# A decoder layer's feed-forward: f sums made on VectorE, operand loads further ahead, and some up-projection weights in pairs of slots

## The chip, the cores and the metric
One core of a Trainium2 chip runs the whole kernel. The metric is the device time of one execution in microseconds (us), median of several runs. The engines are named as in the profile: PE (TensorE matmul), PEld (its weight loads), DVE (VectorE), ACT (ScalarE), POOL (GpSimd, here mostly an issuer of DMAs) and SP (SyncE, here only an issuer of DMAs).

## The reference
One decoder layer on 512 tokens, model width 2048, all in float32. Its last part is what the change touches:

```
x = x + gate_a * mixers(h)                        # attention part, not touched
h = RMSNorm(x) * (1 + scale_f) + shift_f
u = h @ w_up                                      # 2048 -> 2 x 5632
conv = b_conv + sum_j w_conv[j] * shift(u, 2 - j) # causal, three taps
f = silu(conv[:, :5632]) * conv[:, 5632:]
out = x + gate_f * (f @ w_down)                   # 5632 -> 2048
```

## The kernel before
Activations lie feature-major: a tile has 128 features on the partitions and the 512 tokens as columns. Every float32 factor is split into a high and a low part in float32r (`split`: ACT copies into hi, line 114; DVE subtracts, lo = x - hi, line 115), and a product is three matmuls: hi by hi, hi by lo, lo by hi.

**The seven products.** Most of both projections goes through `seven` (lines 919 to 1055). A "pair" of output tiles is computed as a 2x2 block product in seven products in place of eight, on four weight blocks (11, 21, 22, 12) and seven operand sets of the activations (`r11 t3 t2 r21 t1 t4 r22`), each 256 tokens wide. One product is one step of `3*K` matmuls of 128x128 by 128x256: K = 8 in the up projection, 6 or 5 in the down projection. The steps run in the order p1, p7, p6, p2, p5, p4, p3. A step's preparation (`p1` and so on) is emitted two steps ahead of its matmuls: load weight blocks (SP, line 930), combine them (DVE, `comb`, line 941), split the result into one of three hi/lo buffers. After the matmuls an `e` function empties the bank: e1, e7, e6, e3 copy on ACT (`copy`, line 949 in the up projection, 947 in the down projection), e2, e5, e4 add on DVE (`plus`, lines 955 and 953). PE accumulates over several steps in one bank, so PE's p4 and p3 wait for e2 and e5. In program order the weight blocks and s3, the temporary of p7, come out of a queue of five raw buffers (`rawq`): a pair takes L11, L21, s3, L22, L12 and gives s3 back first, then L11 and L21 (p5), L22 (p4), L12 (p3). So L21 of a pair is loaded into the buffer that held L11 of the pair before, and L22 into the one that held L22.

The order of instructions on each engine is not the program's order alone: a scheduler with a model of the engines places an instruction where it believes its inputs to be there. On the chip each engine then works through its queue in that order, and so does SP with the DMAs that it issues.

**Up projection and f.** Four blocks of f are made directly, then 40 pairs by `seven` (`work`, line 1498). After a pair, `ffn_out` applies the convolution (ACT line 1340, DVE lines 1341 and 1342), silu and the product (DVE line 1435) and calls `f_out` (line 1352), which stores what the seven operand sets of the down projection need. Per two blocks j, j+1 it makes negated copies on ACT (lines 1362, 1372) and issues 14 DMAs of 128 KB on POOL: seven plain stores (lines 1363 to 1367, 1373, 1374) and seven that add in DRAM (line 1359).

**Down projection.** It runs in four stages c = 0 to 3 of 6, 6, 5, 5 K-blocks (`DH`), eight pairs each. A stage needs seven operand sets, which `load_set` (line 1448) loads from DRAM on SP (line 1454) and `split_set` (line 1457) splits. `ahead(left)` is called after every step, and it decides when: it splits if `2*need + 8` slots are free, and it keeps at most two sets loaded. A set takes three slots when loaded and six when split. All these tiles, as well as the tiles of the `e` functions and of `f_out`, come from one pool of 81 slots of 128x512 in first-in first-out order (`get`, `put`); during the up projection 64 of them hold h and its sums. Stages 0 to 2 add their result to x1 in DRAM (POOL, line 1506). In stage 3 x1 is loaded (line 1514, `plus()` of `down_pair`), DVE adds it while emptying the bank (line 945), and SP stores the output (line 1508).

Of the kernel before, what the change touches and what calls it, by code (L numbers as in the profile page):

```python
# [10 lines left out]
F32 = mybir.dt.float32  # L11
# [20 lines left out]
def trunk_layer_kernel(  # L32
# [880 lines left out]
    class Pair:  # L913


        def __init__(self, rs, load, fin, K=KH, scale=None, plus=None):
            self.rs, self.load, self.fin, self.K, self.scale, self.plus = rs, load, fin, K, scale, plus

    def seven(work, pairs_of_banks, hook=None):
        def pair_steps(n, p):  # L920
            bx, by = pairs_of_banks[n % len(pairs_of_banks)]
            X, Y, Z = bx[:, :HT], by[:, :HT], by[:, HT:]
            L, E = {}, {}
            W = p.K * P
            g1, g2 = p.scale or (None, None)
            r11, r21, r22, t1, t2, t3, t4 = p.rs

            def load(blk):
                t = rawq.popleft()
                SP.dma_start(t[:, :W], p.load(blk))  # L930
                return t

            def hilo(t):
                i = cnt["wt"] % NH
                cnt["wt"] += 1
                hi, lo = hi_b[i][:, :W], lo_b[i][:, :W]
                split(hi, lo, t[:, :W])
                return hi, lo

            def comb(o, a, b, op):  # L940
                V.tensor_tensor(o[:, :W], a[:, :W], b[:, :W], op)  # L941

            def copy(o, b, g, x):
                if x is not None:
                    V.scalar_tensor_tensor(o, b, g, x, op0=ALU.mult, op1=ALU.add)
                elif g is not None:
                    A.activation(o, b, AF.Copy, scale=g)  # L947
                else:
                    A.activation(o, b, AF.Copy)

            def plus(o, b, g, x):
                if g is not None:
                    V.scalar_tensor_tensor(o, b, g, x, op0=ALU.mult, op1=ALU.add)
                else:
                    V.tensor_tensor(o, b, x, ALU.add)  # L955

            def p1():
                L[11] = load(0)
                L[21] = load(1)
                x = p.plus() if p.plus else (None, None)  # L960
                E["x"] = x
                for i in range(2):
                    for h in range(2):
                        E[f"x{i + 1}{h}"] = None if x[i] is None else x[i][:, h * HT:(h + 1) * HT]
                return hilo(L[11])

            def p7():
                s3 = rawq.popleft()
                comb(s3, L[21], L[11], ALU.subtract)
                r = hilo(s3)  # L970
                rawq.append(s3)
                L[22] = load(3)
                return r

            def p6():
                comb(L[21], L[21], L[22], ALU.add)
                comb(L[11], L[21], L[11], ALU.subtract)
                r = hilo(L[11])
                L[12] = load(2)
                return r  # L980

            def p2():
                return hilo(L[12])

            def p5():
                r = hilo(L[21])
                comb(L[12], L[12], L[11], ALU.subtract)
                rawq.append(L[11])
                rawq.append(L[21])
                return r  # L990

            def p4():
                r = hilo(L[22])
                rawq.append(L[22])
                return r

            def p3():
                r = hilo(L[12])
                rawq.append(L[12])
                return r  # L1000

            def e1():
                E["s"] = get()
                copy(E["s"][:, :HT], X, g1, E["x10"])

            def e7():
                copy(E["s"][:, HT:], Y, g2, E["x21"])

            def e6():
                E["s6"] = get()  # L1010
                copy(E["s6"][:, :HT], X, g2, E["x20"])

            def e2():
                E["u1"] = get()
                plus(E["u1"][:, :HT], Z, g1, E["s"][:, :HT])

            def e5():
                E["u2"] = get()
                plus(E["u2"][:, HT:], X, g2, E["s"][:, HT:])
                put(E["s"])  # L1020

            def e4():
                plus(E["u2"][:, :HT], Y, g2, E["s6"][:, :HT])
                put(E["s6"])

            def e3():
                copy(E["u1"][:, HT:], X, g1, E["x11"])
                if p.plus:
                    put(*E["x"])
# [317 lines left out]


    KINDS = ("r11", "t3", "t2", "r21", "t1", "t4", "r22")
    f_d = {n: [dram.tile([P, HT], F32, name=f"f{n}_{i}") for i in range(NF_ // 2)] for n in KINDS}  # L1350

    def f_out(j, t):
        i = j // 2
        q1, q2 = t[:, :HT], t[:, HT:]
        neg = get()
        n1, n2 = neg[:, :HT], neg[:, HT:]

        def add(n, v):
            G.dma_start(f_d[n][i], v, accum_op=ALU.add)

        if j % 2 == 0:
            A.activation(neg, t, AF.Copy, scale=-1.0)
            G.dma_start(f_d["t1"][i], q2)
            G.dma_start(f_d["t4"][i], q2)
            G.dma_start(f_d["t2"][i], q1)
            G.dma_start(f_d["t3"][i], q2)
            G.dma_start(f_d["r11"][i], q1)
            add("t1", n1)
            add("t4", n1)
            add("t2", n2)  # L1370
        else:
            A.activation(n2, q2, AF.Copy, scale=-1.0)
            G.dma_start(f_d["r21"][i], q1)
            G.dma_start(f_d["r22"][i], q2)
            add("t4", q1)
            add("t2", q2)
            add("t3", n2)
            add("t4", n2)
        put(t, neg)


    tsum = [[], [], [], []]
# [65 lines left out]
    def load_set():  # L1448
        c, n = todo.popleft()
        ts = []  # L1450
        for i in range(DH[c]):
            if i % 2 == 0:
                ts.append(get())
            SP.dma_start(ts[-1][:, (i % 2) * HT:(i % 2 + 1) * HT], f_d[n][base[c] + i])
        coming.append((c, n, ts))

    def split_set():
# [21 lines left out]

    SPARE = 8  # L1480

    def up_hook(q, n):
        last = q - (n - 7)
        if last == 0:
            for t in h2[:KH]:
                put(*t)
        elif last in (1, 2, 4, 5):
            for t in tsum[{1: 2, 2: 1, 4: 0, 5: 3}[last]]:
                put(*t)
        elif last == 6:  # L1490
            for t in h2[KH:]:
                put(*t)
        ahead(n - q)


    all_banks = [(bank[2 * i], bank[2 * i + 1]) for i in range(4)]
    rs = operands(h2, tsum)
    work = [Pair(rs, lambda blk, i=i: w_ups[i, blk], ffn_out(i)) for i in range(NF_ - 4)]
    n_up = len(work) * 7

    def down_pair(c, j):
        def fin(u1, u2):
            for i, u in enumerate((u1, u2)):
                n = 2 * j + i
                if c < len(DH) - 1:
                    G.dma_start(x1_d[n], u, accum_op=ALU.add)  # L1506
                else:
                    SP.dma_start(out[n * P:(n + 1) * P, :], u)
            put(u1, u2)

        def plus():
            ts = [get(), get()]
            for i in range(2):
                G.dma_start(ts[i], x1_d[2 * j + i])
            return ts

        o = ops[c]
        return Pair(tuple(o[n] for n in ("r11", "r21", "r22", "t1", "t2", "t3", "t4")),
                    lambda blk: w_downs[c][j, blk], fin, K=DH[c],
                    scale=(mod[:, 80 + 2 * j:81 + 2 * j], mod[:, 81 + 2 * j:82 + 2 * j]),  # L1520
                    plus=plus if c == len(DH) - 1 else None)

    work += [down_pair(c, j) for c in range(len(DH)) for j in range(KD // 2)]

    def hook(q, n):
# [3 lines left out]
        c, r = divmod(q - n_up, 56)  # L1529
        if r >= 49:  # L1530
            put(*held_by[c][KINDS[r - 49]])
        ahead(0 if (coming or todo or [(0,)])[0][0] == c else 56 - r)

    seven(work, all_banks, hook)

# [55 lines left out]
```

## Time and profile before

| what | value |
|---|---|
| median of 3 runs | 2755.28 us (2752.21 to 2761.14) |
| the profiled execution | 2751.13 us, of which the traced span is 2749.4 us |
| mean granted TensorE clock in it | 0.986 of full speed |
| busy share of the span: PE, DVE, ACT, POOL | 96%, 78%, 46%, 16% |
| moved by DMA | 484.52 MB, of it 112.83 MB on the queue that POOL issues to |

Times in the views count from the start of the span. A row of the timeline has start, duration, engine, line, operation, output<-input and count; in square brackets stands how long the engine was idle ahead of it and what ended that. A row of the groups has the count after x, then total busy time, the mean of one in ns, and after the bar the idle time ahead of such instructions. A row of the waits has who waited for whom, total us, times, longest us. Durations of neighbouring instructions on one engine overlap somewhat; the spacing of their starts is what each costs in the queue.

### The profile page before, as it was taken

How to read it: one execution, taken by the hardware profiler on the slowest of the kernel's cores; microseconds unless marked ns; L12 is line 12 of the kernel's file. 1: busy time of each engine (PE TensorE's matmuls, PEld its weight loads, DVE VectorE, ACT ScalarE, POOL GpSimd, SP SyncE). 2: the span in 40 equal slices, each digit the busy share in tenths (PEclk: the TensorE clock that was granted, in tenths of full speed). 3: DMA queues.
4: the chain of work that ended last, by engine and by line, in shares of the span. 5: the costliest groups of instructions: out<-in, count | busy, mean ns of one | idle time of the engine just before them, and what ended most of it. 6: DMA issues, size and time to landing. Idle time of an engine off the chain costs nothing.

```text
span 2749.4 us, 45335 instructions
## 1 busy us (share of the span) xinstructions
PE 2633.1 (96%) x17200; PEld 2360.8 (86%) x17200; DVE 2154.1 (78%) x3427; ACT 1278.1 (46%) x1979; POOL 443.2 (16%) x715
## 2 busy tenths in 40 slices
PE   6999999998999999999999999999999989898999
PEld 5777687778997767788789999999999988898989
DVE  7977967698888658863868888888888887777788
ACT  4333434334454465222644555555555564545443
POOL 1001011110032222100132222222222221010120
PEclk8999999999999999999999999999999999999999
DMA  9943137665685588952355555555556576656674
GB/s 340 340 146 104 29 113 219 206 196 161 200 257 163 191 261 293 335 169 92 131 142 150 142 152 148 143 157 142 142 156 165 144 218 144 181 138 166 140 203 128
DMA packets 254574, 484.52 MB, mean 176 GB/s; under 512 B 27306, under 2 KB 108100, under 8 KB 254356
## 3 DMA queue, kind: packets, MB, share of 16 engines
q1 hardware_dynamic: 194452, 368.79, 42.9%
q0 software_dynamic: 59872, 112.83, 16.8%
q8 instruction: 134, 2.20, 0.3%
q14 instruction: 84, 0.69, 0.1%
q10 hardware_dynamic: 32, 0.01, 0.0%
HBM read 397.11 MB, written 84.41 MB: 175 GB/s over the span
## 4 chain that ended last, share of the span: by engine, by line
PE 56%; issue 19%; DMA 13%; DVE 9%; POOL 2%; ACT 2%; SPq 0%; DVEq 0%; POOLq 0%; ACTq 0%
PE bank L118 9%; PE bank L119 9%; PE bank L120 9%; PE bank L1050 8%; PE bank L1051 8%; PE bank L1052 8%; DMA raw<-in_w_ups 6%; DVE wlo L115 3%; DMA slot<-in_w_ada 2%; DVE raw L941 2%; POOL x L1506 1%; DMA raw<-in_w_ada 1%; ACT whi L114 1%; DMA gate<-slot 1%; PE bank L1194 1%
## 5 line engine op out<-in xcount | busy, mean ns | idle before, releaser
L1050 PE MATMUL bank<-slot,whi 128*128 128x256 f32 x3920 | 1116.0, 285 | 77.9 <-ACT slot L947 27.9
L1051 PE MATMUL bank<-slot,whi 128*128 128x256 f32 x3920 | 1108.1, 283 | 0.4 <-DVE slot L115 0.4
L1052 PE MATMUL bank<-slot,wlo 128*128 128x256 f32 x3920 | 1100.2, 283 | 2.0 <-DVE wlo L115 2.0
L1050 PEld LDWEIGHTS bank<-slot,whi 128*128 128x128 f32 x3920 | 746.7, 191 | 95.9 <-DVE slot L955 36.0
L114 ACT ACTIVATE whi<-raw 128x1024 fp32r<-128x1024 f32 (+2 forms) x560 | 531.8, 951 | 561.6 <-PE bank L1051 386.4
L1051 PEld LDWEIGHTS bank<-slot,whi 128*128 128x128 f32 x3920 | 745.1, 190 | 0.7 <-DVE slot L115 0.6
L1052 PEld LDWEIGHTS bank<-slot,wlo 128*128 128x128 f32 x3920 | 741.9, 190 | 2.8 <-DVE wlo L115 2.6
L115 DVE TENSOR_TENSOR wlo<-raw,whi 128x1024 fp32r<-128x1024 f32 (+2 forms) x560 | 606.8, 1086 | 80.4 <-ACT whi L114 78.0
L941 DVE TENSOR_TENSOR raw<-raw,raw 128x1024 f32<-128x1024 f32 (+2 forms) x320 | 348.5, 1089 | 143.9 <-DMA raw<-in_w_ups 109.6
L106 ACT ACTIVATE whi<-raw 128x1024 fp32r<-128x1024 f32 (+4 forms) x182 | 187.4, 1031 | 397.1 <-PE bank L120 205.8
L107 DVE TENSOR_TENSOR wlo<-raw,whi 128x1024 fp32r<-128x1024 f32 (+4 forms) x182 | 215.7, 1186 | 145.3 <-ACT whi L106 143.4
L119 PE MATMUL bank<-wlo,slot 128*128 128x512 f32 (+2 forms) x768 | 297.6, 388 | 0.9 <-DVE wlo L107 0.9
L118 PE MATMUL bank<-whi,slot 128*128 128x512 f32 (+2 forms) x768 | 290.3, 391 | 4.4 <-ACT slot L385 3.9
L120 PE MATMUL bank<-whi,slot 128*128 128x512 f32 (+2 forms) x768 | 293.3, 386 | 0.0
L118 PE MATMUL bank<-slot,whi 128*128 128x512 f32 (+1 forms) x656 | 261.2, 405 | 3.1 <-ACT slot L1331 2.3
L119 PE MATMUL bank<-slot,whi 128*128 128x512 f32 (+1 forms) x656 | 263.1, 402 | 0.7 <-DVE slot L687 0.7
L120 PE MATMUL bank<-slot,wlo 128*128 128x512 f32 (+1 forms) x656 | 257.7, 401 | 0.0
L118 PEld LDWEIGHTS bank<-whi,slot 128*128 128x128 f32 x768 | 146.0, 190 | 35.8 <-ACT slot L385 4.0
L723 DVE SCALAR_TENSOR_TENSOR slot<-slot,c_act,slot 128x512 f32<-128x512 f32 x203 | 149.0, 746 | 32.6 <-DMA slot<-in_w_ada 31.4
L119 PEld LDWEIGHTS bank<-wlo,slot 128*128 128x128 f32 x768 | 146.3, 191 | 30.0 <-DVE wlo L107 1.4
L120 PEld LDWEIGHTS bank<-whi,slot 128*128 128x128 f32 x768 | 144.9, 189 | 29.2 <-issue 0.5
L118 PEld LDWEIGHTS bank<-slot,whi 128*128 128x128 f32 (+1 forms) x656 | 123.2, 188 | 33.9 <-issue 2.8
(292 smaller groups left out, 2813.2 us busy)
## 6 DMA issues: line engine op xcount, KB each, us to landing
slot<-in_w_ada SPq DMA_DIRECT2D x344, 256.0 KB, 5.5
raw<-in_w_ups SPq DMA_DIRECT2D x160, 512.0 KB, 4.4
ft<-slot POOLq DMA_DIRECT2D x242, 128.0 KB, 4.6
raw<-in_w_in SPq DMA_DIRECT2D x50, 512.0 KB, 3.6
raw<-in_w_down SPq DMA_DIRECT2D x64, 384.0 KB, 3.9
raw<-in_w_down SPq DMA_DIRECT2D x64, 320.0 KB, 3.0
raw<-in_w_gs SPq DMA_DIRECT2D x32, 512.0 KB, 3.8
raw<-in_w_o SPq DMA_DIRECT2D x32, 512.0 KB, 4.7
```

The costliest lines, as they stand in the source:

```text
L106: A.activation(hi, raw[:, :w], AF.Copy)
L107: V.tensor_tensor(lo, raw[:, :w], r32(hi), ALU.subtract)
L114: A.activation(dst_hi, src, AF.Copy)
L115: V.tensor_tensor(dst_lo, src, r32(dst_hi), ALU.subtract)
L118: PE.matmul(o, lh, rh, start=first, stop=False)
L119: PE.matmul(o, lh, rl, start=False, stop=False)
L120: PE.matmul(o, ll, rh, start=False, stop=last)
L723: V.scalar_tensor_tensor(acc, ts[i], c_act[:, k:k + 1], acc, op0=ALU.mult, op1=ALU.add)
L941: V.tensor_tensor(o[:, :W], a[:, :W], b[:, :W], op)
L1050: PE.matmul(o, wh[:, ks], rh, start=first and k == 0, stop=False, skip_group_check=True)
L1051: PE.matmul(o, wh[:, ks], rl, start=False, stop=False, skip_group_check=True)
L1052: PE.matmul(o, wl[:, ks], rh, start=False, stop=last, skip_group_check=True)
```

## The change
Four things change, all in the last part of the kernel.

1. `f_out` keeps the first of two blocks in its slot, and at the second makes the four needed sums on DVE (four subtractions of 128x256). It then stores plainly: one DMA of 128 KB at the first block, three of 256 KB at the second. The negated copies on ACT and the DMAs that add go. The loads pick their half out of the wider tiles.
2. `ahead`: of a coming stage's sets up to three are loaded ahead of their split (one only, in stage 0 while 15 or fewer slots are free); it begins 50 steps ahead instead of 35. Sets are split early every fourth step, at most four, and otherwise in the last eight steps. Sets of stage c+2 no longer start within stage c. The spare count is 6 for stage 0, 8 otherwise.
3. For the first 34 of the 40 pairs of the up projection (`slots=i < NF_ - 10`), s3 and L12 live in two slots of 512 columns each, and no longer in a raw buffer. What is done on them (the load, two of the four combinations, three of the seven splits) becomes two instructions of half the width. L11, L21 and L22 stay in the five raw buffers.
4. In stage 3 the `e` functions copy on ACT as in the other stages, and two DVE additions of 128x512 per pair add x1 in `fin`.

```
     def f_out(j, b):
         i = j // 2
         if j % 2 == 0:
             first_of.append(b)
             G.dma_start(f_d[i][0], b[:, :HT])
             return
         a = first_of.pop()
         p, q = get(), get()
         V.tensor_tensor(p[:, :HT], a[:, HT:], a[:, :HT], ALU.subtract)
         V.tensor_tensor(p[:, HT:], b[:, HT:], p[:, :HT], ALU.subtract)
         V.tensor_tensor(q[:, :HT], a[:, HT:], b[:, HT:], ALU.subtract)
         V.tensor_tensor(q[:, HT:], b[:, :HT], p[:, HT:], ALU.subtract)
         for n, t in ((1, b), (2, p), (3, q)):
             G.dma_start(f_d[i][n], t)
         put(a, b, p, q)
```
```
-    def ahead(left):
-        c = todo[0][0] if todo else coming[0][0] if coming else None
-        if c is None or left > 35 or left > 8 and left % 2:
+    made = [0]
+    def ahead(left, last):
+        c = (coming or todo or [(9,)])[0][0]
+        if c > last or left > 50:
             return
-        if coming and len(free) >= 2 * need(coming[0][0]) + SPARE:
+        n, spare = need(c), 8 if c else 6
+        if coming and coming[0][0] <= c and len(free) >= 2 * n + spare and (left <= 8 or left % 4 == 0 and made[0] < 4):
+            made[0] = (made[0] + 1) % 7
             split_set()
-        if todo and todo[0][0] <= c and len(coming) < 2 and len(free) >= need(todo[0][0]) + SPARE:
+        while todo and todo[0][0] <= c and len(coming) < (3 if c or len(free) > 15 else 1) and len(free) >= n + spare:
             load_set()
```
```
             def p7():
-                s3 = rawq.popleft()
+                s3 = new(p.slots)
                 comb(s3, L[21], L[11], ALU.subtract)
                 r = hilo(s3)
-                rawq.append(s3)
+                done(s3)
                 L[22] = load(3)
...
-                L[12] = load(2)
+                L[12] = load(2, p.slots)
```
```
+        def fin(*us):
+            for i, (n, u) in enumerate(zip(ns, us)):
+                if x1:
+                    V.tensor_tensor(u, u, x1[i], ALU.add)
+                    SP.dma_start(out[n * P:(n + 1) * P, :], u)
+                else:
                     G.dma_start(x1_d[n], u, accum_op=ALU.add)
```

More of the change, by code (lines that the diff above doesn't have):

```diff
@@ L926, in pair_steps, with new, done, part @@
             r11, r21, r22, t1, t2, t3, t4 = p.rs
-            def load(blk):
-                t = rawq.popleft()
-                SP.dma_start(t[:, :W], p.load(blk))
+            def new(slots=False):
+                if slots:
+                    return [(get(), 0, T), (get(), T, W)]
+                return [(rawq.popleft(), 0, W)]
+            def done(t):
+                if len(t) == 1:
+                    rawq.append(t[0][0])
+                else:
+                    put(*(x[0] for x in t))
+            def part(t, lo, hi):
+                for b, x, y in t:
+                    if x <= lo and hi <= y:
+                        return b[:, lo - x:hi - x]
+            def cuts(*ts):
+                return [(x, y) for _, x, y in max(ts, key=len)]
+            def load(blk, slots=False):
+                t = new(slots)
+                for b, x, y in t:
+                    SP.dma_start(b[:, :y - x], p.load(blk)[:, x:y])
                 return t
@@ L936, in hilo, with copy @@
                 hi, lo = hi_b[i][:, :W], lo_b[i][:, :W]
-                split(hi, lo, t[:, :W])
+                for x, y in cuts(t):
+                    split(hi[:, x:y], lo[:, x:y], part(t, x, y))
                 return hi, lo
             def comb(o, a, b, op):
[L941 to L946, printed above, removed]
+                for x, y in cuts(o, a, b):
+                    V.tensor_tensor(part(o, x, y), part(a, x, y), part(b, x, y), op)
+            def copy(o, b, g):
+                if g is not None:
                     A.activation(o, b, AF.Copy, scale=g)
@@ L987, in p5 @@
                 comb(L[12], L[12], L[11], ALU.subtract)
-                rawq.append(L[11])
-                rawq.append(L[21])
+                done(L[11])
+                done(L[21])
                 return r
@@ L993, in p4 @@
                 r = hilo(L[22])
-                rawq.append(L[22])
+                done(L[22])
                 return r
@@ L998, in p3 @@
                 r = hilo(L[12])
-                rawq.append(L[12])
+                done(L[12])
                 return r
@@ L1026, in e3 @@
             def e3():
-                copy(E["u1"][:, HT:], X, g1, E["x11"])
-                if p.plus:
-                    put(*E["x"])
+                copy(E["u1"][:, HT:], X, g1)
                 p.fin(E["u1"], E["u2"])
```

82 lines of the change are left out of this document (26 added, 56 removed).

## The prediction
> **What bounds the kernel now.** I read the page first, then PE's timeline from the first matmul of the up projection's pairs to the last of the down projection, to see how far each stage is from back-to-back matmuls.
>
> ```profile
> PE 2633.1 (96%) x17200; PEld 2360.8 (86%) x17200; DVE 2154.1 (78%) x3427; ACT 1278.1 (46%) x1979; POOL 443.2 (16%) x715
> ...
> 1407.54 0.28 PE L1050 MATMUL bank<-slot,whi 128*128 128x256 f32 x1
> ...
> 1952.73 0.28 PE L1050 MATMUL bank<-slot,whi 128*128 128x256 f32 x1
> ...
> 1958.63 0.28 PE L1052 MATMUL bank<-slot,wlo 128*128 128x256 f32 x1
> ...
> 2111.99 0.29 PE L1051 MATMUL bank<-slot,whi 128*128 128x256 f32 x1
> ...
> 2242.18 0.28 PE L1051 MATMUL bank<-slot,whi 128*128 128x256 f32 x1
> 2266.93 0.28 PE L1051 MATMUL bank<-slot,whi 128*128 128x256 f32 x1
> 2319.18 0.29 PE L1050 MATMUL bank<-slot,whi 128*128 128x256 f32 x1
> 2364.47 0.29 PE L1050 MATMUL bank<-slot,whi 128*128 128x256 f32 x1
> 2387.84 0.41 PE L1052 MATMUL bank<-slot,wlo 128*128 128x256 f32 x1
> 2408.29 0.28 PE L1050 MATMUL bank<-slot,whi 128*128 128x256 f32 x1
> 2502.44 0.28 PE L1050 MATMUL bank<-slot,whi 128*128 128x256 f32 x1
> 2521.93 0.28 PE L1051 MATMUL bank<-slot,whi 128*128 128x256 f32 x1
> 2542.79 0.28 PE L1050 MATMUL bank<-slot,whi 128*128 128x256 f32 x1
> 2626.16 0.28 PE L1050 MATMUL bank<-slot,whi 128*128 128x256 f32 x1
> 2644.90 0.28 PE L1051 MATMUL bank<-slot,whi 128*128 128x256 f32 x1
> 2745.48 0.28 PE L1052 MATMUL bank<-slot,wlo 128*128 128x256 f32 x1
> ```
>
> PE is 96% busy, but a matmul is shown 0.28 us long while the next starts earlier, so the spacing of starts is the measure. The 51 starts from 1952.73 to 1958.63 are 0.118 us apart. A pair in the up projection is 168 matmuls, so 19.82 us at the least; a down pair 126 (14.87) or 105 (12.39). Counting matmuls from 1407.54 gives the other rows: the end of pair 34 of the up projection, the start of stage 0, and inside stages 0 to 2 the ends of the first pair, of the fourth in stage 0, and the start of the last (a row may be off by one matmul). Over the floor lie:
>
> - up, pairs 1 to 34: 704.5 - 673.9 = 30.6 us, or 0.90 a pair (20.72 each);
> - up, pairs 35 to 40: 130.2 - 118.9 = 11.3;
> - stage 0: 145.7 - 119.0 = 26.7, of which the first pair has 9.9, the next three 7.6, the last 8.5;
> - stage 1: 134.1 - 119.0 = 15.1 (first pair 5.6, last 4.6, between 4.9);
> - stage 2: 123.0 - 99.1 = 23.9 (first 8.5, last 6.3, between 9.0);
> - stage 3: 100.7 - 99.1 = 1.6.
>
> So 109 us is all that this part can give back, and the change touches what lies behind them. Next, who waits in the up projection (waits view of 1370 to 2225 us, then DVE's, PE's and POOL's timelines of one pair and the table by stretches):
>
> ```profile
> DVE raw L941 <- DMA raw<-in_w_ups: 109.6, 77, 3.6
> PE bank L1050 <- DVE slot L955: 19.6, 30, 1.9
> ...
> 1950.72 0.69 DVE L1435 TENSOR_TENSOR slot<-slot,slot 128x512 f32<-128x512 f32 x1
> 1951.33 1.22 DVE L941 TENSOR_TENSOR raw<-raw,raw 128x1024 f32<-128x1024 f32 x1
> 1952.46 1.22 DVE L115 TENSOR_TENSOR wlo<-raw,whi 128x1024 fp32r<-128x1024 f32 x1
> 1954.26 1.23 DVE L115 TENSOR_TENSOR wlo<-raw,whi 128x1024 fp32r<-128x1024 f32 x1 [0.58 <-ACT whi L114]
> 1957.58 1.23 DVE L941 TENSOR_TENSOR raw<-raw,raw 128x1024 f32<-128x1024 f32 x1 [2.09 <-DMA raw<-in_w_ups]
> 1958.72 0.42 DVE L955 TENSOR_TENSOR slot<-bank,slot 128x256 f32<-128x256 f32 x1
> ...
> 1961.03 1.23 DVE L941 TENSOR_TENSOR raw<-raw,raw 128x1024 f32<-128x1024 f32 x1 [0.76 <-DMA raw<-in_w_ups]
> ...
> 1959.19 0.38 PE L1050 MATMUL bank<-slot,whi 128*128 128x256 f32 x1 [0.28 <-DVE slot L955]
> ...
> 1958.40 0.85 POOL L1359 DMA_DIRECT2D ft<-slot x1 [2.82 <-DMA ft<-slot]
> ...
> 1600.00:1800.00 200.00, 197.91 (x1654) 196.23 (x1653) 169.39 (x187) 106.78 (x147) 50.01 (x70) 1.00 0.57 149
> ```
>
> This is the loop. At 1951.33 DVE makes p5's L12 - L11, the last reader of L11, and so frees the buffer into which SP loads the next pair's L21. Its landing ends DVE's wait at 1957.58, 5.0 us after that combination ended. At 1961.03 the same happens with L22, whose buffer p4's split (1954.26) had freed. DVE's queue is in order, so e2 (1958.72) stands behind a wait it has nothing to do with, and PE's p4 waits for e2. In the stretch 1600 to 1800 DVE is busy 169.39 of 200 us, 17.55 of a pair's 20.72: it idles 3.17 a pair, nearly all of it such waits.
>
> In the down projection the waits are of another kind (waits of 2225 to 2750, groups by form, two rows of ACT and PE):
>
> ```profile
> ACT slot L114 <- DMA slot<-fr: 14.4, 7, 3.2
> ACT slot L114 <- DMA x<-slot: 14.1, 6, 3.3
> ...
> L115 DVE TENSOR_TENSOR wlo<-raw,whi 128x768 fp32r<-128x768 f32 x111 | 105.2, 955 | 33.0 <-ACT whi L114 31.3
> L115 DVE TENSOR_TENSOR slot<-slot,slot 128x512 fp32r<-128x512 f32 x52 | 35.0, 687 | 23.5 <-ACT slot L114 19.7 <-DMA x<-slot 3.6
> L953 DVE SCALAR_TENSOR_TENSOR slot<-bank,mod,slot 128x256 f32<-128x256 f32 x96 | 45.9, 479 | 12.1 <-PE bank L1052 12.1
> ...
> 2372.43 0.63 ACT L114 ACTIVATE slot<-slot 128x512 fp32r<-128x512 f32 x1 [3.22 <-DMA slot<-fr]
> ...
> 2374.21 0.39 PE L1050 MATMUL bank<-slot,whi 128*128 128x256 f32 x1 [2.55 <-ACT slot L947]
> ```
>
> ACT stands in its queue waiting for an operand set that was loaded too shortly ahead (3.22 us), or for a slot that a store to x1 still reads; the bank copies behind it come late, and PE waits 2.55 us.
>
> **Part by part: weights in slots (34 pairs).** With s3 and L12 out of `rawq`, a pair takes three of five buffers. Then L11 and L21 come into buffers free since two pairs ago, so the 2.09 wait goes. L22 comes into L11's buffer of the pair before, freed at 1951.33 and not at 1954.26. What is late next is L22: landing 5.0 us after the combination, with on DVE in between two splits (1.13 each, by the starts 1951.33 and 1952.46) and s3 (two halves, 0.61 each by 1950.72 to 1951.33), 3.5 us. So L22 can cost between 0 and 1.5 us of idle DVE; I take 0.8, since the combination may also run earlier with L12 there in time.
>
> DVE's added work: five instructions become two halves. By starts a half costs 0.61 and a whole 1.13, so +0.09 each, 0.45 a pair; by durations 2 x 0.69 - 1.23 = 0.15 each, 0.75 a pair. I take 0.45, the starts being what a queue pays. [...]
>
> `f_out` adds four subtractions of 128x256 per two pairs (0.42 each by line 955's row), 0.84 a pair on the mean. DVE then needs 17.55 + 0.45 + 0.84 = 18.84, with 0.8 of idle 19.6: just under PE's 19.82. In pairs with the sums it is 19.7 ahead of any idle, so some stalls stay. I leave 0.30 us a pair of today's 0.90: **-20 us** (between 0 and -30).
>
> ACT loses two negations per two pairs and gains three half splits a pair; it is busy 106.78 of 200 us, so nothing either way. POOL issues 4 DMAs for 14 per two blocks and no chain of adds (2.82 us wait in the row above); nobody on PE's path waits for POOL, so 0.
>
> What the slots add as waits: SP's load of L12 and DVE's s3 now wait for a slot, with the next pair's L11, L21, L22 queued behind on SP and e2, e5 on DVE. Counting `get` and `put` through the code, a slot that an f store has read comes back after at least 10 steps (28 us). Today the last add is issued at 1958.40, 7.7 us after the product at 1950.72, so stores are over long before: 0. In the last five up pairs stage 0's first sets take slots, and the same count falls to 4 steps (11 us): e2 and e5 of three pairs may wait. Against this stand one set less to split in the last seven steps and shorter f stores: 0 for pairs 35 to 40, between -5 and +8.
>
> **Operand sets.** A down pair with K = 6 needs on DVE 11 x 0.955 (splits and combinations) + 3 x 0.479 = 11.9 us of PE's 14.87, and a set 3 x 0.687 = 2.1. By the code's order six sets are split in the last pair of stage 0 today (three of stage 1, three of stage 2): 11.9 + 12.4 = 24.3, and that pair took 23.4. So it is DVE's pair, and not only a wait for loads. After the change four are left there: 20.2. The other three go behind steps 8, 12 and 16, where a pair has 3.0 to spare, loaded at least two steps (4 us) ahead into slots that were free for 8 steps or more, while today the sets of steps 22 to 28 reuse slots after 1 to 7 steps. I take:
>
> - stage 0: first pair -2 (six sets instead of seven in the last up steps), next three 7.6 to 3 (-4.6), last 8.5 to 5 (-3.5): -10;
> - stage 1: first 5.6 to 2, between -1, last -2: -6.6;
> - stage 2: first 8.5 to 3, between 9.0 to 4, last -1.3 (four sets instead of three, but loaded in time): -11.8.
>
> **-28.4 us**, between -8 (only the removed splits count) and -45 (only DVE's overload stays).
>
> **Stage 3 and the end.** Four bank copies a pair go from DVE to ACT, and two additions of 128x512 come: inside the stage, 1.6 us over its floor, 0. At the very end the addition stands between the last copy and the store: +0.7 (0 to +1.4, if both additions queue).
>
> Sum: -20 - 28.4 + 0.7 = -47.7 on the profiled execution's 2751.1, so 2703.4. The runs' median lies 4.2 above that execution, and I carry that over: **2707 us**.
>
> **Rivals.** (a) The up projection gains nothing: L22's wait is as long as L21's was, and DVE's 18.84 + 2 = 20.8 is today's pair. For it: the order on DVE is fixed by a model that thinks loads faster than they are. Against: 3.5 us of work now stands in the gap. Time 2727. (b) The stage boundaries are DVE's work and the splits only move: down gains 12, 2724. (c) Both, or loads that in fact don't run further ahead because slots are short: about 2748, no change. (d) Slower: DVE sets the up projection's pace. If its idle of 3.17 a pair stays in whole (L22 and slots in place of L21 and L22), a pair costs 18.84 + 3.17 = 22.0, +1.29 x 34 = +44, and with -28.4 and +0.7 in the rest 2771. It decides from an idle of 1.9 a pair on, where the up projection starts to lose; above 2.7 the kernel does. Against it: L21's load no longer depends on the pair ahead.
>
> **How the numbers follow.** Forecast 0.57 (2707), (a) 0.18, (b) 0.12, (c) 0.05, (d) 0.08. The low end has up -30, down -45: 2680. The high end takes in (a), (b) and most of (c): 2748. What differs by under 0.3% (8 us) a measurement of this kernel can't tell from no change: faster 0.87, same 0.05, slower 0.08.
>
> **What would show it.** Up pairs of 20.0 to 20.2 us; DVE's waits for in_w_ups under 45 us in place of 110, and those left on the load of L22; PE's waits for line 955's additions under 8 us; no waits of DVE or SP for f stores in the first 33 pairs; last pairs of stages 0 and 1 under 20 and 18.5 us; ACT waiting under 5 us for f loads and for x1 stores. Wrong would be: DVE above 95% with up pairs over 20.7 us, or long waits for slots.

## The result and the profile after

The changed kernel takes **2720.0 us** (median of 4 runs, 2717.0 to 2724.5) beside 2753.7 of the kernel before: 0.988 of its time, with a 95% interval of 0.985 to 0.991. The profiled execution is 2718.77 us, its span 2716.3. The forecast was 2707, within a range of 2680 to 2748, and faster at 0.87: a gain of 48 us, where 34 were measured.

First the page's line of busy times and PE's timeline of the changed kernel. The starts answer to those shown of before: pair 1 of the up projection, the end of pair 34, the start of stage 0, the end of its first pair, the start of its last, and so on to the last matmul. Lines have moved: the three matmuls are now L1065 to L1067 (before L1050 to L1052), the weight load L952 (L930), the combinations L965 (L941), the bank copies L969 and L971 (L947 and L949), the additions of `e2`, `e5`, `e4` L975 and L977 (L953 and L955).

```profile
PE 2620.4 (96%) x17200; PEld 2351.7 (87%) x17200; DVE 2184.6 (80%) x3669; ACT 1285.3 (47%) x2069; POOL 270.5 (10%) x495
```
```profile
1408.58 0.28 PE L1065 MATMUL bank<-slot,whi 128*128 128x256 f32 x1
...
2094.91 0.28 PE L1066 MATMUL bank<-slot,whi 128*128 128x256 f32 x1
...
2222.39 0.28 PE L1066 MATMUL bank<-slot,whi 128*128 128x256 f32 x1
...
2244.41 0.28 PE L1066 MATMUL bank<-slot,whi 128*128 128x256 f32 x1
...
2341.66 0.28 PE L1065 MATMUL bank<-slot,whi 128*128 128x256 f32 x1
2358.57 0.28 PE L1066 MATMUL bank<-slot,whi 128*128 128x256 f32 x1
...
2474.34 0.28 PE L1065 MATMUL bank<-slot,whi 128*128 128x256 f32 x1
2491.82 0.28 PE L1066 MATMUL bank<-slot,whi 128*128 128x256 f32 x1
2509.05 0.28 PE L1065 MATMUL bank<-slot,whi 128*128 128x256 f32 x1
...
2592.38 0.29 PE L1066 MATMUL bank<-slot,whi 128*128 128x256 f32 x1
2607.83 0.28 PE L1066 MATMUL bank<-slot,whi 128*128 128x256 f32 x1
2624.08 0.41 PE L1066 MATMUL bank<-slot,whi 128*128 128x256 f32 x1
...
2711.88 0.28 PE L1067 MATMUL bank<-slot,wlo 128*128 128x256 f32 x1
```

The differences of these starts, beside those of before, give where the 33.1 us of the span went:

| part | before | after | difference | forecast |
|---|---|---|---|---|
| ahead of the pairs | 1407.5 | 1408.6 | +1.0 | none |
| up, pairs 1 to 34 | 704.4 | 686.3 | -18.1 | -20 |
| up, pairs 35 to 40 | 130.2 | 127.5 | -2.7 | 0 |
| stage 0 | 145.7 | 136.2 | -9.5 | -10 |
| stage 1 | 134.1 | 133.2 | -0.9 | -6.6 |
| stage 2 | 123.0 | 116.0 | -7.0 | -11.8 |
| stage 3 | 100.7 | 104.2 | +3.5 | 0 |
| after the last matmul | 3.9 | 4.4 | +0.5 | +0.7 |

PE's idle time at the border of the up projection and stage 0 (in the changed kernel 1.9 us, ahead of 2224.74) is counted to stage 0, here and in the kernels below. The largest gain fits its forecast almost exactly. The waits do not fit it (waits of the changed kernel, 1370 to 2200 us, then those of SP's queue from 1410 to 2090):

```profile
DVE slot L965 <- DMA raw<-in_w_ups: 36.1, 26, 3.6
DVE raw L965 <- DMA raw<-in_w_ups: 20.9, 30, 2.4
PE bank L1065 <- DVE slot L977: 2.9, 7, 1.0
```
```profile
SPq L952 <- DVE slot L1357: 297.6, 46, 12.5
```

DVE's 109.6 us have become 57.0, but the longer part, 36.1 us, is s3 in its slots, so still the wait that the slots were to remove. And SP stands 298 us before loads of L12, for a slot that the convolution (L1357) still uses; the prediction had named this wait and taken it as 0. One pair tells what each is worth, in SP's and DVE's timelines:

```profile
1602.42 0.33 SPq L952 DMA_DIRECT2D raw<-in_w_ups  x1
1615.33 3.47 SPq L952 DMA_DIRECT2D slot<-in_w_ups  x2
1619.03 1.46 SPq L952 DMA_DIRECT2D raw<-in_w_ups  x2
1622.69 0.33 SPq L952 DMA_DIRECT2D raw<-in_w_ups  x1
```
```profile
1601.17 1.22 DVE L115 TENSOR_TENSOR wlo<-raw,whi 128x1024 fp32r<-128x1024 f32 x1
...
1607.65 0.69 DVE L965 TENSOR_TENSOR slot<-raw,raw 128x512 f32<-128x512 f32 x1 [1.40 <-DMA raw<-in_w_ups]
...
1618.32 0.68 DVE L965 TENSOR_TENSOR slot<-slot,raw 128x512 f32<-128x512 f32 x1
```

What ends s3's wait at 1607.65 is the landing of the load issued at 1602.42, the L21 that s3 reads. This load did not stand behind L12's. It went out as a split on DVE (1601.17) ended, the last reader of the raw buffer that the load goes into. All 26 waits of s3 are like this one: SP had stood for L21's raw buffer, 2.2 us in the median, and the load took 5.4 us to land. So the raw buffers are still what DVE waits for. s3 meets them because it now runs early: it is s3 of the coming pair, and L12 - L11 of the pair ahead, which stands before it in the program, follows 10 us later (1618.32 is its second half). Before, s3 needed a raw buffer itself; that the scheduler moves it forward because it no longer does is argued, not tested.

From 1602.75 to 1615.33 SP issues nothing: it stands 12.5 us at the load of L12. That looks worse than it is. The raw load behind it, at 1619.03, went out as L12 - L11 ended (1619.00), which freed its own buffer. Of the 32 raw loads that stand right behind a load of L12, 30 went out within 0.06 us after that end; one was 0.4 us late and one 2. Before, SP stood 412 and 220 us for raw buffers in about the same stretch (1410 to 2110), so the length of its waits says little.

So the total was right to half a per cent, and the reason for it was in doubt. The question for the experiments: which of the four parts gave the 18 us of the up projection?

### The profile page after: what moved, and what is told of

Its sections match the earlier page's. It is cut to its first block, busy times and chain, and to the rows that moved or that the text cites. A ratio compares the mean times of both kernels' runs of the same rounds, so it can differ in the third digit from the quotient of the medians.

```text
span 2716.3 us, 45517 instructions
## 1 busy us (share of the span) xinstructions
PE 2620.4 (96%) x17200; PEld 2351.7 (87%) x17200; DVE 2184.6 (80%) x3669; ACT 1285.3 (47%) x2069; POOL 270.5 (10%) x495
## 3 DMA queue, kind: packets, MB, share of 16 engines
q0 software_dynamic: 36640, 92.63, 11.7%
HBM read 397.11 MB, written 64.23 MB: 170 GB/s over the span
## 5 line engine op out<-in xcount | busy, mean ns | idle before, releaser
L1065 PE MATMUL bank<-slot,whi 128*128 128x256 f32 x3920 | 1109.9, 283 | 49.4 <-ACT slot L969 17.0
L1067 PE MATMUL bank<-slot,wlo 128*128 128x256 f32 x3920 | 1101.6, 282 | 8.3 <-DVE wlo L115 8.2
L1065 PEld LDWEIGHTS bank<-slot,whi 128*128 128x128 f32 x3920 | 743.4, 190 | 62.4 <-ACT slot L969 22.2
L1067 PEld LDWEIGHTS bank<-slot,wlo 128*128 128x128 f32 x3920 | 739.9, 189 | 10.8 <-DVE wlo L115 10.3
L114 ACT ACTIVATE whi<-raw 128x1024 fp32r<-128x1024 f32 (+2 forms) x458 | 424.6, 928 | 500.1 <-PE bank L1066 385.5
L115 DVE TENSOR_TENSOR wlo<-raw,whi 128x1024 fp32r<-128x1024 f32 (+2 forms) x458 | 482.1, 1056 | 61.7 <-ACT whi L114 59.6
L965 DVE TENSOR_TENSOR raw<-raw,raw 128x1024 f32<-128x1024 f32 (+2 forms) x252 | 264.8, 1051 | 61.8 <-DMA raw<-in_w_down 33.3
L118 PEld LDWEIGHTS bank<-whi,slot 128*128 128x128 f32 x768 | 145.9, 190 | 36.1 <-ACT slot L385 4.3
L114 ACT ACTIVATE whi<-slot 128x512 fp32r<-128x512 f32 x204 | 127.0, 630 | 79.4 <-PE bank L1066 63.8
```

Source lines behind the costliest of these rows:

```text
L114: A.activation(dst_hi, src, AF.Copy)
L115: V.tensor_tensor(dst_lo, src, r32(dst_hi), ALU.subtract)
L118: PE.matmul(o, lh, rh, start=first, stop=False)
L965: V.tensor_tensor(part(o, x, y), part(a, x, y), part(b, x, y), op)
L1065: PE.matmul(o, wh[:, ks], rh, start=first and k == 0, stop=False, skip_group_check=True)
L1067: PE.matmul(o, wl[:, ks], rh, start=False, stop=last, skip_group_check=True)
```

## The experiments

**Each part alone, and the change without part 4.** The theory was the prediction's: the gain of the up projection belongs to part 3. The rival: it belongs to part 1, in which POOL's DMAs that add in DRAM disappear.

`p1_sums`, `p2_ahead` and `p3_slots` are the kernel before with the hunks of the diff for `f_out` and `load_set`, for `ahead`, and for `new`, `done`, `part`, `cuts` alone. In `no_p4` the hunk of `fin` is undone:

```
 p1_sums:   f_out as after (sums on DVE, plain stores), the loads pick their half
 p2_ahead:  ahead(left, last) as after
 p3_slots:  slots=i < NF_ - 10, s3 = new(p.slots), L[12] = load(2, p.slots)
 no_p4:     after, with  copy(o, b, g, x)  adding x1 on DVE again
```

> Kernel before with part 1 alone (f sums on DVE, plain stores). Theory (each part's share stands in its own stage; DVE's idle time in the up projection is waiting, so it has room): 0.84 us more DVE work a pair, of which the 3.17 us of idle time takes most; up pairs 20.7 as before, the whole between -3 and +8 us. Rival (DVE paces the up projection, its waits stay whatever is added): +0.84 x 40 = +34 us, up pairs 21.5. Second rival (the fewer DMAs make the weight loads land sooner): up pairs 20.3, -15 us.

> Kernel before with part 2 alone (loads further ahead, other places for the splits). Theory (the gain of the down projection is this part's): stages 0 to 2 at 136, 133 and 116 us as in the changed kernel instead of 146, 134 and 123, up projection unchanged: -15 to -19 us. Rival (what the down projection gained came from the plain f stores being over earlier): stages as before, within 4 us of no change.

> Kernel before with part 3 alone (s3 and L12 in slots for 34 pairs), f_out with its adding DMAs as before. Theory (the raw buffers were the up projection's stall): first 34 pairs at 686 to 690 us instead of 704, the rest as before: -14 to -18 us. Rival (the slots only pay together with part 1, since f stores that add hold their slots longer and the weights of L12 wait for them): first 34 pairs 700 or more, gain under 5 us.

> Changed kernel with part 4 undone (x1 added while the bank is emptied, as before). Theory (stage 3 lost 3.5 us because its first pair waits for a weight load that stands behind others on SP, not through part 4): stage 3 still at 103 to 105 us, the end 0.5 us shorter, -0.5 us against the changed kernel. Rival (the copies on ACT and the late additions cost it): stage 3 back at 100.7, -4 us.

Measured, in one session with 14 runs of before at 2754.16 us:

| kernel | us | ratio to before (95%) | up 1 to 34 | stages 0 to 2 | stage 3 | end |
|---|---|---|---|---|---|---|
| before | 2754.2 | 1 | 704.4 | 402.8 | 100.7 | 3.9 |
| part 1 alone | 2711.3 | 0.983 (0.981 to 0.986) | 676.9 | 394.5 | 100.9 | 3.9 |
| part 2 alone | 2749.6 | 0.998 (0.996 to 0.999) | 714.7 | 389.9 | 103.7 | 3.9 |
| part 3 alone | 2777.9 | 1.007 (1.005 to 1.009) | 735.2 | 400.2 | 99.7 | 4.0 |
| after without part 4 | 2715.9 | 0.985 (0.982 to 0.988) | 685.6 | 386.8 | 103.1 | 3.8 |

The columns of stages come from one profiled execution each, the times from all runs. Part 1 alone gives 43 us, more than the whole change; its second rival named the cause, at 15 us. Part 3 alone costs 24, which neither its theory nor its rival had. For part 1, DVE's waits from 1370 us to the end of the up pairs, the stretch 1600 to 1800 (columns as in the prediction's row: stretch, length, busy time and instructions of PE, PEld, DVE, ACT, POOL, then clock, DMA share, GB/s), and from the page the row of POOL's queue q0 (packets, MB, share of 16 engines) and that of the weight loads (KB each, median us to landing):

```profile
DVE raw L941 <- DMA raw<-in_w_ups: 51.4, 68, 3.6
```
```profile
1600.00:1800.00 200.00, 200.00 (x1689) 199.98 (x1688) 178.27 (x209) 107.55 (x140) 10.81 (x20) 1.00 0.40 131
```
```profile
q0 software_dynamic: 36640, 92.63, 11.7%
...
raw<-in_w_ups SPq DMA_DIRECT2D x160, 512.0 KB, 3.6
```

And the same two rows of the page of before:

```profile
q0 software_dynamic: 59872, 112.83, 16.8%
...
raw<-in_w_ups SPq DMA_DIRECT2D x160, 512.0 KB, 4.4
```

The weight load lands after 3.6 us instead of 4.4, and a pair takes 19.91 us instead of 20.72, which is PE's floor of 19.82 but for 0.09. DVE is 89% busy and still waits 51 us for loads, and PE doesn't notice: it has no idle in 200 us. In part 3 alone, the waits of the same kind (1370 us to the end of the up pairs) and those of SP (1410 to 2090 us):

```profile
DVE slot L965 <- DMA raw<-in_w_ups: 71.5, 31, 4.0
DVE raw L965 <- DMA raw<-in_w_ups: 44.0, 39, 3.2
PE bank L1074 <- DVE slot L979: 33.7, 33, 2.9
```
```profile
SPq L952 <- DVE slot L1366: 177.8, 31, 12.7
```

115.5 us of DVE's waits for 109.6 before, and PE waits 33.7 for the additions instead of 19.6. The slots do not remove the wait: in all 31 waits of s3 here, too, the load of L21 had itself waited on SP for its raw buffer, 2.1 us in the median. Two of the theory's claims fall here: that the slots give the gain, and that POOL's work is worth nothing.

Without part 4 the stages hardly differ, 2.4 of stage 3's 3.5 us stay, and the end is 0.6 shorter. Part 2 alone shows 3.0 of stage 3's loss (103.7), so most of it belongs to part 2. In the up projection part 2 alone has 10 us more than before, where it issues nothing; its runs spread over 19 us (2737.5 to 2756.2), those of part 1 alone over 1.2 (2710.6 to 2711.8), so a single profile of a kernel that keeps the adding DMAs tells its up projection only within some 10 us, as an estimate from these spreads.

**Is it the adding, the bytes, or the negations on ACT?** Part 1 takes away three things at once. `adds_plain` keeps all but the adding; `adds_out` drops these seven DMAs per two blocks; `p1_adds` puts seven adding DMAs, to scratch, on top of part 1, without the negations.

```
 adds_plain:   G.dma_start(f_d[n][i], v)                          # was accum_op=ALU.add
 adds_out:     pass                                               # in place of it
 p1_adds:   +  for n, v in enumerate((...seven halves of p, q, b...)):
            +      G.dma_start(extra[n], v, accum_op=ALU.add)
```

> Kernel before, the seven DMAs per two blocks that add in DRAM made plain stores of the same size (the adding is left out, so the operand sets are wrong). Theory (an adding DMA reads and writes its target and so loads the DMA engines more than a plain store; it slows the weight loads beside it, 4.4 us to landing against 3.6 with part 1 alone): weight loads land in 3.7 to 4.0 us, first 34 up pairs at 680 to 690 us, -15 to -25 us. Rival 1 (the number of DMAs or the bytes stored matter, not the adding): up stays at 700 to 705. Rival 2 (the negations on ACT in front of the splits were the cost): up stays at 700 to 705 too, and p1_adds then tells it from rival 1.

> Part 1 alone, with seven DMAs of 128 KB per two blocks added that add slot halves to scratch tiles in DRAM nobody reads (extra work; the first time they store). DVE's sums and the missing negations stay as in part 1 alone. Theory (traffic of the adding DMAs is what part 1 removed): weight loads back at 4.2 us or more, first 34 up pairs back at 697 to 715 us instead of 677, +20 to +35 us against part 1 alone. Rival (removed negations or the sums filling DVE's gaps gave the gain): up stays at 677 to 682.

> Kernel before with the seven adding DMAs per two blocks left out altogether (the sums are not formed); the seven plain stores of 128 KB, ACT's negations and the rest stay. With those made plain stores the first 34 up pairs took 689 us, with part 1 alone 677. Theory (what is left of the difference is traffic too): 677 to 681 us, weight loads landing in 3.5 to 3.7 us, -28 to -35 us. Rival (what is left is the negations on ACT or the short DMAs): 685 to 689.

| kernel | us | ratio to before (95%) | up 1 to 34 |
|---|---|---|---|
| before: 7 adding, 7 plain | 2752 | 1 | 704.4 |
| 14 plain (`adds_plain`) | 2732.6 | 0.993 (0.990 to 0.996) | 689.2 |
| 7 plain, the others left out (`adds_out`) | 2720.2 | 0.988 (0.986 to 0.990) | 678.0 |
| part 1 and 7 adding (`p1_adds`) | 2763.9 | 1.004 (1.002 to 1.007) | 707.7 |

Each ratio is to the runs of before in its own session (medians 2751.8 and 2752.2); the 704.4 is of the profile shown at the start. `p1_adds` runs from 2752.1 to 2778.1, and its profile is of the fastest run.

From the pages of `adds_plain`, `adds_out` and `p1_adds`, in this order:

```profile
q0 software_dynamic: 45088, 112.83, 13.8%
...
raw<-in_w_ups SPq DMA_DIRECT2D x160, 512.0 KB, 3.8
```
```profile
q0 software_dynamic: 37696, 92.64, 11.9%
...
raw<-in_w_ups SPq DMA_DIRECT2D x160, 512.0 KB, 3.6
```
```profile
q0 software_dynamic: 58144, 112.83, 16.5%
...
raw<-in_w_ups SPq DMA_DIRECT2D x160, 512.0 KB, 4.5
```

Of the 26 us between before and `adds_out` in these pairs, 15 go with the adding and 11 with the seven transfers as such, to within the 10 us by which a single profile of before can be off; the runs of the three kernels don't overlap. ACT's negations stay in both, so they are not it; and `p1_adds`, which has none, is back at 707.7 and 4.5 us. Nor do the stores hold up other engines by their slots: in the kernel before, from 1370 to 2225 us, ACT waits once for such a store, 1.9 us, and SP 5.5 us. The price of the adding can be read from the shares: the same 154 transfers of 128 KB take 13.8% x 2728.5 - 11.9% x 2718.5 = 53 us of 16 engines when plain, and 16.8% x 2749.4 - 323.5 = 138 us when they add, 2.6 times as much. `p1_adds` gives 16.5% x 2750.3 - 11.7% x 2709.0 = 137 again. The theory's ground, that an adding transfer also reads its target, no run shows: the page of before, with the adding, and that of the changed kernel, without it, both count 397.11 MB read from HBM. What the runs show is the time.

**What the slots do beside the other parts, and SP's queue.** `no_slots` is after with `slots=False`. `l12_pool` issues the loads of L12 on POOL's queue, so that SP never stands at them. They test whether SP's order is what part 3 loses by.

```
 no_slots:  slots=False
 l12_pool:  q = G if slots else SP;  q.dma_start(b[:, :y - x], p.load(blk)[:, x:y])
```

> Changed kernel with slots=False for all pairs, so parts 1, 2 and 4 without part 3. Theory (part 3 costs in the up projection what it was to bring): first 34 up pairs at 677 to 679 us instead of 686, last six at 125 to 127, down projection as in the changed kernel (489), whole 2702 to 2710, -10 to -15 us against the changed kernel. Rival (slots only hurt beside the adding DMAs, and what is left above part 1 alone comes from part 2 in the up projection): first 34 at 685 or more, no gain.

> Changed kernel, the loads of L12 into slots issued on POOL's queue instead of SP's. Theory (part 3 costs because SP, in order, stands at L12's load until the convolution of the pair before has read its slot, 298 us of such waits, and L11, L21, L22 queue behind it): DVE's waits for in_w_ups fall from 57 to under 20 us, first 34 up pairs at 677 to 681 us, -5 to -9 us. Rival (the cost is DVE's: ten instructions of half width for five, and their place in the queue): first 34 pairs stay at 684 to 690.

`no_slots`: 2722.1 us, 0.989 (0.987 to 0.991), pairs 1 to 34 in 678.5. `l12_pool`: 2720.8, 0.988 (0.986 to 0.991), 682.4. So beside parts 1, 2 and 4 the slots cost 7.8 us in the up projection, and moving L12 off SP brings back 3.9 of them, by one profile each. Runs of these kernels spread over 7 to 9 us, so the 3.9 is not clear of noise; that the slots cost something is, by part 3 alone. DVE's waits from 1370 us to the end of the up pairs, without slots and then with L12 on POOL's queue (L966 is the combination, moved by a line):

```profile
DVE raw L965 <- DMA raw<-in_w_ups: 49.7, 61, 3.7
```
```profile
DVE raw L966 <- DMA raw<-in_w_ups: 39.7, 29, 2.9
DVE slot L966 <- DMA raw<-in_w_ups: 6.0, 8, 1.3
```

With L12 off SP, s3's wait falls from 36.1 to 6.0. The other wait, nearly all of it the addition of L22, rises from 20.9 to 39.7. That is the late L22 which the prediction had expected, and it takes the place of the wait that went: both together are 45.7 us, not under the 20 expected. So the theory, that SP's order makes DVE wait, does not hold: most of the wait stays, and in the changed kernel none of the loads that s3 waited for stood behind L12's. What makes up the 7.8 us was not separated. Two rows point at something: DVE's added work, 618.60 us of 684 (1410 to 2094) against 611.84 of 678 without slots, and later landings, though no f store adds. Here are the raw loads with slots, then without:

```profile
raw<-in_w_ups SPq DMA_DIRECT2D x126, 512.0 KB, 4.4
```
```profile
raw<-in_w_ups SPq DMA_DIRECT2D x160, 512.0 KB, 3.6
```

So the time to landing tells of the f stores only between kernels that issue their loads alike, as the four of the table above do.

The total of `no_slots` was expected at 2702 to 2710 and did not improve: stage 0 takes 146.8 and stage 1 139.3, for 136.2 and 133.2 after, though both kernels run the same code there (the profile is of its slowest run, 5.5 us above the median). The traces show one cause. From stage 0 to the end of stage 2, PE's matmuls come in the same order in both, and the order on ACT, DVE and SP differs only at neighbouring places near the start. One of these is a split of an operand set that stands two places earlier in ACT's queue. ACT is idle 3.8 us ahead of it (2245.32) and PE then waits 5.0 us for a bank copy; that pair takes 23.4 us for 17.4. The rest of stage 0 and the 6 us of stage 1 come with the same order and stay open.

**Why the down projection gave half.** In the changed kernel, from 2222 to 2610 us:

```profile
DVE raw L965 <- DMA raw<-in_w_down: 25.6, 24, 2.0
DVE slot L115 <- DMA x<-slot: 16.7, 8, 3.0
PE bank L1065 <- ACT slot L969: 16.7, 17, 2.3
...
ACT slot L114 <- DMA x<-slot: 11.2, 7, 2.8
ACT slot L114 <- DMA slot<-f: 4.7, 1, 4.7
```

ACT's waits for f loads fell to 4.7 us as forecast. The waits for slots that a store to x1 still reads did not: DVE's are new (16.7 for 3.6). The theory: sets are split into result slots given back a moment ago, and giving these back one pair later frees the stages. The rival: the time only turns into another wait.

```
 hold:   late.append((*us, *x1));  if len(late) > 1: put(*late.pop(0))     # was put(*us, *x1)
 ns_hold: the same on no_slots        p1_hold: the same on p1_sums, SPARE = 6
```

> Changed kernel; in the down projection a pair's two result slots go back into the pool one pair later (the places of the splits in the program stay the same). Theory (what the earlier splits were to gain is lost because they are put into slots that the adding store to x1 still reads; ACT and DVE wait 28 us for such stores): those waits fall under 6 us, stages 0 to 2 from 386 to 362 to 372 us, -13 to -23 us against the changed kernel. Rival (DVE's overload in the last pairs and the weight loads hold the stages; the waits for the stores only show first): stages within 5 us of 386.

> The same with slots=False for all pairs of the up projection (parts 1, 2 and 4, and the late return of slots). Theory: up projection at 678 and 126 us as without slots, stages 0 to 2 at 365 to 378 instead of 402, whole 2688 to 2700 and so the fastest of all. Rival: stages stay at 395 to 405, whole 2715 to 2722.

> Part 1 alone, with the late return of slots and a spare count of 6 instead of 8, so that the splits stay at the same places. Theory (waits for x1 stores are 15 us there, waits for f loads 20): only the former go, stages 0 to 2 from 394.5 to 384 to 391, -4 to -10 us against part 1 alone. Rival: within 3 us of part 1 alone.

| kernel | us | ratio to before (95%) | up 1 to 34 | stages 0, 1, 2 |
|---|---|---|---|---|
| after | 2720.0 | 0.988 (0.985 to 0.991) | 686.3 | 136.2, 133.2, 116.0 |
| `hold` | 2717.5 | 0.987 (0.985 to 0.990) | 683.6 | 141.3, 130.5, 118.9 |
| `no_slots` | 2722.1 | 0.989 (0.987 to 0.991) | 678.5 | 146.8, 139.3, 116.0 |
| `ns_hold` | 2714.0 | 0.986 (0.983 to 0.988) | 676.3 | 138.7, 131.7, 118.4 |
| part 1 alone | 2711.3 | 0.983 (0.981 to 0.986) | 676.9 | 142.2, 134.2, 118.1 |
| `p1_hold` | 2725.4 | 0.989 (0.987 to 0.992) | 677.1 | 145.5, 138.3, 124.0 |

In `hold` DVE's waits for the stores are gone from the list, and the stages take 390.7 us, not less than after's 385.4. Its waits from 2222 to 2610 us:

```profile
DVE raw L965 <- DMA raw<-in_w_down: 30.1, 23, 4.7
...
ACT slot L114 <- DMA x<-slot: 10.4, 6, 2.4
```

The theory falls: 16.7 us of waits went and the stages did not get shorter. Without slots in the up projection the same edit gives 13 us in the stages, and on part 1 alone it loses 13, where neither theory nor rival had a loss. A mechanism that holds for all three was not found. The edit also did more than it was meant to: in the traces of `hold`, `ns_hold` and `p1_hold` SP's loads of the stages come in another order than in the kernels they are made from. So the late return of slots was not tested by itself. What can be said is that stages of the same code differ by 10 us or more between kernels that differ elsewhere, in one profiled execution each, and that the place of a single split can make 6 us of it.

The lowest median of all is that of part 1 alone: 2711.3 us, below before in the same session, and below every run of the changed kernel (its slowest run 2711.8, the changed kernel's fastest 2717.0, though in another session). `ns_hold` and the change without part 4 are not told from it: their intervals overlap. But parts 2 and 4 cost beside it: with them (`no_slots`) the time is 2722.1, with 7.6 us more in stages 0 to 2 and 4 more in stage 3.

## Why the prediction was right, and where it was not

The number held because two errors met: a gain that was costed at nothing, and a gain that was a loss. That the up projection's -18.1 comes so near to the forecast's -20 is luck. The total, 2720, lies nearer to rival (b)'s 2724 than to 2707.

- **Part 1 at zero: the step that failed.** "Nobody on PE's path waits for POOL, so 0" asked who waits for POOL's engine, and not what its transfers do to the loads of the others. The rows for it stood in the prediction: the adding DMA in flight in the shown pair, the DMA share of 0.57, the 5.0 us from a combination to the next landing, taken as given. Measured with part 1 alone: 27.5 us in pairs 1 to 34, 43 in all. The experiments show the adding and the seven transfers as the cause.
- **Part 3 at -20: wrong in sign.** It is +7.8 in the up projection beside the other parts, and part 3 alone costs 24 us. The step is "Then L11 and L21 come into buffers free since two pairs ago, so the 2.09 wait goes". The buffers are those of two pairs ago, as counted. But s3 ran ahead of its place in the program, and L21's buffer came free only some 5 us before it (1602.39 and 1607.65 in the pair shown). Rival (a) had named the order on DVE as the reason, and saw it in L22's load alone; that the model behind the order thinks loads faster than they are no run shows, only that s3 waited 26 times for a load issued some 5.4 us before. The prediction also named SP's wait for L12's slot and priced it at 0. The wait came, 298 us long, and so did the sign of being wrong that was named for it; but the loads behind it had no buffers to go into either, so that price is not what failed. The sign "no waits for f stores" nearly held (3.0 us on SP, 1410 to 2090) and told nothing of this.
- **L22's wait** (0 to 1.5 us a pair, 0.8 taken): 13.8 us from 1410 to 2090, or 0.4 in each of the 34 pairs; with L12 off SP's queue 31.9, or 0.9.
- **DVE's work.** By the stretch of 1600 to 1800, which stands below with rows of DVE's timeline, DVE needs 179.50 of 200 us, 18.1 of a pair's 20.19; 18.84 was forecast. The halves are spaced 0.60 us (1611.47 to 1612.07), as taken from the starts. By durations a split in halves takes 0.14 us more than a whole one (two of 0.68 for one of 1.22), by the starts 0.06 (two of 0.60 for one of 1.14, from 1608.26 to 1609.40). DVE's idle time is 2.1 us a pair, not the 3.17 of rival (d), and the pair takes 20.19 us, not 22.0.

```profile
1600.00:1800.00 200.00, 199.25 (x1674) 198.42 (x1674) 179.50 (x259) 109.46 (x169) 10.75 (x20) 1.00 0.38 128
```
```profile
1608.26 1.22 DVE L115 TENSOR_TENSOR wlo<-raw,whi 128x1024 fp32r<-128x1024 f32 x1
1609.40 0.68 DVE L115 TENSOR_TENSOR wlo<-slot,whi 128x512 fp32r<-128x512 f32 x1
...
1611.47 0.68 DVE L115 TENSOR_TENSOR wlo<-slot,whi 128x512 fp32r<-128x512 f32 x1
1612.07 0.68 DVE L965 TENSOR_TENSOR slot<-raw,raw 128x512 f32<-128x512 f32 x1
```

- **Operand sets at -28.4:** -17.4 in the changed kernel, -12.9 with part 2 alone. Not all of the 17.4 is part 2's: part 1 alone has -8.3 in these stages, and parts 1, 2 and 4 without the slots have -0.7. So part 2's own share is not settled. Stage 0 was right to half a us; the terms that were mis-sized are stage 1 (-0.9 for -6.6) and stage 2 (-7.0 for -11.8). The last pairs of stages 0 and 1 did fall, to 16.9 and 17.5 us from 23.4 and 19.5, as the signs named for them said. But the two pairs ahead of them rose to 17.0 and 17.7 in stage 0, where they had 14.9 and 15.4: DVE's splits moved, and part of their time with them. That is rival (b)'s mechanism, at some 60% of the forecast's gain. (Rival (c), as (a) and (b) together, comes to 2744, not 2748.)
- **Stage 3 at 0:** +3.5, nearly all in its first pair (16.25 us for 13.32), from part 2. **The end at +0.7:** +0.6 between the kernels with and without part 4.

Of the signs, those of the result came true (up pairs 20.19, PE's waits for the additions 2.9, last pairs, ACT's 4.7 for f loads). Those of the cause did not: DVE's waits 57 instead of under 45, most of them not on L22, and ACT's 11.2 for x1 stores. A total that fits is no evidence for the terms.

## What to carry to other kernels

Price a removed transfer by what it does to the loads beside it, also where nobody waits for it: compare landing times with and without it, between kernels that issue their loads alike (here 3.8 us for 4.4 where only the adding went), and measure what a transfer that adds in DRAM costs beside a plain one (here 2.6 times). When a temporary gets buffers of its own, look where the scheduler then puts its instruction: moved forward, it can meet the same late load again (here in 26 waits, 36.1 us). And follow a wait to the load that ended it, and that load to what let it go, before an issuer's long wait is called the cause. When a change has several parts, run each alone: here one part was better than the whole.

## What was unexpected of the hardware

Transfers of the same 20.2 MB took 2.6 times the DMA engines' time when they added in DRAM (138 for 53 us of 16 engines), with 59872 packets on the queue in before for 45088 in `adds_plain`. With the adding, 512 KB loads on another queue landed after 4.4 us in place of 3.8, at a mean DMA share of only 0.57 (before, 1600 to 1800 us).
